# Pooling as a product with a constant band matrix, lambda by a small matmul, and another place for the residual affine

## The chip, the cores and the metric

One core of one Trainium2 chip runs the whole program. The metric is the device time of one execution in microseconds (us); lower is better. The kernel before was run three times for its median, and once more under the hardware profiler.

## The reference

A diffusion backbone of two layers works on 256 latent tokens and 256 context tokens of 1024 channels. Each layer is a half-step SwiGLU feed-forward, a token mixer, and a second feed-forward; after each of them the residual goes through a LayerNorm with gain and bias. Layer 0 mixes with differential attention plus multi-scale pooling, layer 1 with a convolution. What the change touches is in the mixer of layer 0:

```python
lam = exp(sum(lam_q1 * lam_k1)) - exp(sum(lam_q2 * lam_k2)) + lam_init      # one number
z_lat = h_lat @ w_in                       # q, k, v: 512 columns each, then u: 512 columns
# pooling of u, four groups of 128 channels, windows 2, 4, 8, 16 over the tokens:
mean = (csum[hi] - csum[lo]) / (hi - lo)   # windowed mean, clipped at both ends
pooled = mean - u                          # per group
y = pooled @ w_pool[g] * pool_scale
# attention: p_diff = softmax(s0) - lam * softmax(s1);  out = p_diff @ v
```

## The kernel before, in words

Every large product is made three times (mm3, lines 194 to 197: high x high, high x low, low x high), with each operand split into a rounded high part (fp32r) and its remainder. Activations lie split and transposed in XH and XL, as [channel, token]: tokens 0 to 255 are latent, 256 to 511 context. Weights come from HBM as fp32 in 1 MB jobs into three raw buffers (pump_load, queue SP), and each job is cut into pieces of 128x1024 that ScalarE copies to wh and VectorE subtracts to wl (pump_split, lines 132 and 133). Six pairs of wh and wl rotate; wnext (line 136) takes the next piece and asks for those up to five ahead.

The feed-forward ahead of the mixer ends with four blocks of 128 tokens in a row, t = 0, 1 (latent) and 2, 3 (context). Each ends in finish(t), lines 579 to 584: LayerNorm without its gain and bias (they are folded into the next modulation), then to_x, which transposes h[t] on TensorE (tile tra), modulates it on VectorE and ScalarE (xma), and splits it into XH and XL. The second half of each XL split is on GpSimd (line 333). For the latent tokens the gain and bias still have to be applied to the residual h[t] itself: affine(t, 0, 0, pool), put aside in a list (later, line 584) and emitted when flush is called. It loads two rows of 1024 floats to all partitions by GpSimd's own DMA queue, through one buffer, and multiplies and adds them in halves: for two blocks four row loads and eight 128x512 operations, all issued on GpSimd.

The mixer (lines 591 to 822) takes u first: four products of 256 columns (lines 626 to 629) give u as [channel, token], ScalarE copies each into the zero-padded tile UP, and GpSimd forms the windowed sums SA and SB by shifted additions, multiplies with INV (1 / count), subtracts u, and splits the result into PH and PL (lines 630 to 642; the last instruction is called pooled). Lambda (lines 605 to 614) is a product and a reduction on VectorE over a loaded tile lq, then an exponential on ScalarE. Then come, as written, four q heads and two k heads, each with a rotation (rope, lines 644 to 658: ScalarE copy rh, a matmul with perm, VectorE products t1 and t2, a ScalarE copy and a VectorE subtraction), attend(0), the product for v, attend(1), and so on. PH and PL are read much later, by the product with w_pool (lines 769 to 776). flush(pooled) stands at line 805, after attend_out(3).

The order of each engine's queue is made by a planner at build time: on each engine it takes the earliest-written instruction among those that are ready, unless an edge holds one back. tc.issue_after(i) makes such edges: it queues the instructions of its block behind instruction i, those of i's own engine only. (behind_x, line 274, therefore opens it for two anchors, a VectorE and a ScalarE one, to hold both halves of a weight split.) The engines then run their queues strictly in order. Memory of a closed pool is reused: the mixer's pools mp and m2 lie where the feed-forward's pools lay, and their tiles wait for the last reader there.

Of the kernel before, what the change touches and what calls it, by code (L numbers as in the profile page):

```python
# [9 lines left out]
F32 = mybir.dt.float32  # L10
# [6 lines left out]
P = 128  # L17
# [25 lines left out]
CO = {}  # L43
_n = 0
for _name, _w in (("c", 8), ("cc", 8), ("lng", 48), ("lnb", 48), ("cvg", 8), ("cvb", 8), ("bc1", 16), ("bdw", 8),
                  ("psc", 4), ("sub", 1), ("bad", 9 * 8 * DEPTH)):
    CO[_name] = _n
    _n += _w
NCOL = _n
# [3 lines left out]
def body(ctx: ExitStack, tc: tile.TileContext, out, a):  # L53
# [13 lines left out]
    def mmt(name):  # L67
        return mmp.tile([P, 512], F32, tag="mm", name=name)
# [30 lines left out]
    def w_add(src, widths):  # L99
        jobs.append((src, widths))  # L100
# [61 lines left out]
    PARTS4 = ((0, 8), (8, 16), (16, 22))  # L162
    PARTS2 = ((0, 22),)
    add_ffn(0, 0, 4, PARTS4)
    for g in range(2):
        w_add(a["wu"][2 * g:2 * g + 2].rearrange("j p f -> p j f"), (1024, 1024))
    for hd in range(0, NH, 2):
        w_add(a["wqk"][0, hd:hd + 2].rearrange("j p f -> p j f"), (1024, 1024))
    w_add(a["wqk"][1, 0:2].rearrange("j p f -> p j f"), (1024, 1024))
    for hh in range(2):  # L170
        w_add(a["wv"][:, hh * 2048:(hh + 1) * 2048], (1024, 1024))
    w_add(a["wqk"][1, 2:4].rearrange("j p f -> p j f"), (1024, 1024))
# [418 lines left out]
    with ExitStack() as st2:  # L591
        mp = st2.enter_context(tc.tile_pool(name="mp", bufs=1))
        m2 = st2.enter_context(tc.tile_pool(name="m2", bufs=2))
        xmp[:] = m2, 2
        UP = mp.tile([P, 4, 512], F32R, tag="VH", name="UP").bitcast(F32)[:, :, 0:272]
        pool.memset(UP, 0.0)
        cosT = mp.tile([P, SEQ], F32, name="cosT")
        nc.sync.dma_start(cosT, a["cosT"])
        sinT = mp.tile([P, SEQ], F32, name="sinT")
        nc.sync.dma_start(sinT, a["sinT"])  # L600
        perm = mp.tile([P, P], F32, name="perm")
        nc.sync.dma_start(perm, a["perm"])
        INV = m2.tile([P, 4, SEQ], F32, tag="pt", bufs=4, name="INV")
        nc.sync.dma_start(INV, a["inv"].partition_broadcast(P))
        lq = m2.tile([P, 4, 64], F32, tag="rh", name="lq")
        nc.sync.dma_start(lq, a["lam"].partition_broadcast(P))
        lam = mp.tile([P, 4], F32, name="lam")
        dve.tensor_tensor(lq[:, 0:2, :], lq[:, 0:2, :], lq[:, 2:4, :], ALU.mult)
        dve.tensor_reduce(lam[:, 0:2], lq[:, 0:2, :], AX.X, ALU.add)
        act.activation(lam[:, 0:2], lam[:, 0:2], AF.Exp)  # L610

        dve.tensor_tensor(lam[:, 2:3], lam[:, 1:2], lam[:, 0:1], ALU.subtract)
        lam_init = 0.8 - 0.6 * math.exp(-0.3 * 0)
# [4 lines left out]
        def proj(ps, tok0, tok1):  # L618
            wh, wl = wnext()
            for k in range(KT):  # L620
                mm3(ps, wh[:, k * P:(k + 1) * P], wl[:, k * P:(k + 1) * P], XH[:, k, tok0:tok1], XL[:, k, tok0:tok1],
                    k == 0, k == KT - 1)

        SA = m2.tile([P, 4, 272], F32, tag="pt", bufs=4, name="SA")
        SB = m2.tile([P, 4, 272], F32, tag="pt", bufs=4, name="SB")
        for g in range(4):
            psu = mmt(f"u{g}")[:, 0:SEQ]
            proj(psu, 0, SEQ)
            act.copy(UP[:, g, 8:8 + SEQ], psu)
        pool.tensor_tensor(SA[:, :, 0:271], UP[:, :, 0:271], UP[:, :, 1:272], ALU.add)  # L630
        pool.tensor_tensor(SB[:, 1:4, 0:269], SA[:, 1:4, 0:269], SA[:, 1:4, 2:271], ALU.add)
        pool.tensor_tensor(SA[:, 2:4, 0:265], SB[:, 2:4, 0:265], SB[:, 2:4, 4:269], ALU.add)
        pool.tensor_tensor(SB[:, 3, 0:257], SA[:, 3, 0:257], SA[:, 3, 8:265], ALU.add)
        PH = mp.tile([P, 4, SEQ], F32R, tag="PH", name="PH")
        PL = mp.tile([P, 4, SEQ], F32R, tag="PL", name="PL")
        for g, win in enumerate(WINS):
            src = (SA, SB)[g % 2]
            o = 8 - win // 2
            pool.tensor_tensor(INV[:, g, :], src[:, g, o:o + SEQ], INV[:, g, :], ALU.mult)
            pool.tensor_tensor(INV[:, g, :], INV[:, g, :], UP[:, g, 8:8 + SEQ], ALU.subtract)  # L640
# [48 lines left out]
        def attend(hd, between=None):  # L689
# [25 lines left out]
            if between is not None:  # L715
                with tc.issue_after(between().ins):
                    for qt in range(2):
                        turn(hd, qt, es[qt])

        def turn(hd, qt, e):  # L720
            pth, ptl = PT[hd]
            qs = slice(qt * P, (qt + 1) * P)
            tr = trt(f"ptr{hd}{qt}")
            for kt in range(4):
                pe.transpose(tr[:, kt * P:(kt + 1) * P], e[:, 0, kt * P:(kt + 1) * P], ident)
            split(pth[:, :, qs], ptl[:, :, qs], tr.rearrange("p (k q) -> p k q", k=4))

        def attend_out(hd):
            pth, ptl = PT[hd]
# [29 lines left out]
            do_q(hd)  # L759
        do_k(0)  # L760
        do_k(1)
        attend(0)
        do_v()
        attend(1)
        do_k(2)
# [36 lines left out]
        attend_out(2)  # L802
        pooled_half(1)
        attend_out(3)
        flush(pooled)
        for n in range(2):
            for q in range(2):
                wq[q, n] = wnext()
# [236 lines left out]
def _layout(i):  # L1045
    import numpy as np
    f = lambda v: np.asarray(v)
    ar = np.ascontiguousarray
    L = DEPTH
    o = {}  # L1050

    def vec(v):
        return f(v).reshape(-1, P).T

    b_ada = f(i["b_ada"]).reshape(L, 9, D)

    GATES = (2, 5, 8)
    by = lambda b, v: b.reshape(P, 8).T if v in GATES else b.reshape(8, P)
    bad = np.concatenate([by(b_ada[l, v], v).T for l in range(L) for v in range(9)], axis=1)
    o["cols"] = ar(np.concatenate([  # L1060
        vec(i["c"]), vec(i["c_ctx"]), vec(i["ln_g"]), vec(i["ln_b"]), vec(i["conv_ln_g"]), vec(i["conv_ln_b"]),
        vec(i["b_c1"]), vec(i["b_dw"]), vec(i["pool_scale"]), vec(i["subln_g"]), bad], axis=1))
    o["wdw"] = ar(f(i["w_dw"])[0].reshape(TAPS, 8, P).transpose(2, 1, 0).reshape(P, 8 * TAPS))
    x, ctx = f(i["x"])[0], f(i["ctx"])[0]
    o["x"], o["ctx"] = ar(x), ar(ctx)
    o["xT"] = ar(np.stack([v.reshape(SEQ, KT, P).transpose(2, 1, 0).reshape(P, KT * SEQ) for v in (x, ctx)]))
    wa = f(i["w_ada"]).reshape(L, D, 9, D)
    o["wst"] = ar(wa[0, :, 0:2].reshape(2, 4, P, 2, 2, 512).transpose(3, 4, 0, 2, 1, 5).reshape(2, 2, 2, P, 2048))
    wt = wa.transpose(0, 2, 3, 1)
    o["wada"] = ar(np.stack([np.stack([  # L1070
        wt[l, v].reshape(P, 8, D).transpose(1, 0, 2) if v in GATES else wt[l, v].reshape(8, P, D)
        for v in range(9)]) for l in range(L)]))
    o["c_row"], o["cc_row"] = ar(f(i["c"])[0]), ar(f(i["c_ctx"]))
    o["ln_g"], o["ln_b"] = ar(f(i["ln_g"])), ar(f(i["ln_b"]))
# [8 lines left out]
    o["wu"] = ar(wm[:, 1536:].reshape(KT, P, 4, P).transpose(2, 1, 0, 3).reshape(4, P, 1024))  # L1083
# [7 lines left out]
    o["lam"] = ar(np.stack([f(i["lam_" + k])[0] for k in ("q1", "q2", "k1", "k2")]))  # L1091

    f4 = np.float32
    pos = np.arange(SEQ)
    inv = (f4(10000.0) ** (-np.arange(16, dtype=f4) / f4(16))).astype(f4)
    ang = np.stack([(pos // 64).astype(f4)[:, None] * inv, (pos % 64).astype(f4)[:, None] * inv], 1)
    tab = lambda v: ar(np.broadcast_to(v.astype(f4).transpose(1, 2, 0)[None, :, None], (2, 2, 2, 16, SEQ)).reshape(P, SEQ))
    o["cosT"], o["sinT"] = tab(np.cos(ang)), tab(np.sin(ang))
    perm = np.zeros((P, P), f4)
    for m in range(P):  # L1100
        if m % 32 < 16:
            perm[m + 16, m] = -1.0
        else:
            perm[m - 16, m] = 1.0
    o["perm"] = perm
    cnt = np.stack([np.clip(pos - w // 2 + w, 0, SEQ) - np.clip(pos - w // 2, 0, SEQ) for w in WINS])
    o["inv"] = (1.0 / cnt).astype(f4)
    return o


# [14 lines left out]
```

## Time and profile before

| | us |
|---|---|
| median of three runs | 1262.07 (1261.28 to 1267.06) |
| the profiled execution | 1265.42 |
| its span in the profile | 1263.6 |
| TensorE busy in the span | 1213.8 (96%) |
| VectorE busy | 893.3 (71%) |
| ScalarE busy | 520.0 (41%) |
| GpSimd busy | 250.3 (20%) |

Times in the rows are us from the start of the span. PE is TensorE, PEld its weight load, DVE VectorE, ACT ScalarE, POOL GpSimd, SPq the queue that issues most DMAs. In a row of the timeline the bracket at the end says how long the engine had been idle before the instruction, and which instruction ended that. The mixer of layer 0 runs from about 403 to 538.

### The profile page before, as it was taken

The page shows a single profiled execution, that of the slowest core. Times are in us where ns is not written, and L with a number is a line of the kernel's source. Part 1 is how long each engine was busy: PE and PEld are TensorE (multiplying, and loading weights), DVE is VectorE, ACT ScalarE, POOL GpSimd, SP SyncE. Part 2 cuts the span into 40 slices and gives each one's busy share as a digit, 9 for nine tenths or more (in the row PEclk, how much of TensorE's full clock was granted, in tenths as well). Part 3 has the DMA queues.
Part 4 walks back from the last instruction along what each step waited for, and adds up shares of the span by engine and source line. Part 5 has one row for each costly group of instructions (what it writes and reads, how often), then busy time and mean ns, then how long its engine had stood idle before and what let it go on. Part 6 is the DMA issues. An engine that isn't in the chain of part 4 may idle for free.

```text
span 1263.6 us, 17520 instructions
## 1 busy us (share of the span) xinstructions
PE 1213.8 (96%) x6886; PEld 1037.2 (82%) x6886; DVE 893.3 (71%) x1278; ACT 520.0 (41%) x790; POOL 250.3 (20%) x231
## 2 busy tenths in 40 slices
PE   7999999999999899989999999999999979999997
PEld 1788888888887777779998869999879867999985
DVE  6889987733328957787785668888658976775554
ACT  2533122212323535553444443444438853444430
POOL 0010201111003740123000014201016961420000
PEclk9999999999999999989999999999999989999999
DMA  9797788632231452558985649998726042875550
GB/s 366 286 370 252 276 283 291 232 100 99 80 117 67 140 166 67 167 188 299 327 291 184 238 144 333 321 333 307 260 105 240 22 146 117 309 269 176 180 183 34
DMA packets 63748, 264.32 MB, mean 209 GB/s; under 512 B 5937, under 2 KB 6705, under 8 KB 56241
## 3 DMA queue, kind: packets, MB, share of 16 engines
q1 hardware_dynamic: 60128, 251.11, 56.8%
q0 software_dynamic: 3536, 12.09, 3.1%
q8 instruction: 54, 0.88, 0.3%
q14 instruction: 30, 0.24, 0.1%
HBM read 262.10 MB, written 1.08 MB: 208 GB/s over the span
## 4 chain that ended last, share of the span: by engine, by line
PE 84%; DVE 8%; ACT 3%; DMA 2%; issue 1%; POOL 1%; SPq 0%; DVEq 0%; ACTq 0%; POOLq 0%
PE of L197 8%; PE of L196 8%; PE of L195 8%; PE uf L197 8%; PE uf L196 8%; PE uf L195 8%; PE gf L196 7%; PE gf L195 7%; PE gf L197 7%; PE c L197 1%; DVE wl L133 1%; PE c L196 1%; PE c L195 1%; PE pc L986 1%; PE st L519 1%
## 5 line engine op out<-in xcount | busy, mean ns | idle before, releaser
L133 DVE TENSOR_TENSOR wl<-raw,wh 128x1024 fp32r<-128x1024 f32 x298 | 376.5, 1276 | 170.9 <-ACT wh L132 170.0
L132 ACT CAST wh<-raw 128x1024 fp32r<-128x1024 f32 x313 | 321.9, 1048 | 394.7 <-PE of L197 130.0
L197 PE MATMUL uf<-XH,wl 128*128 128x256 f32 (+1 forms) x656 | 205.2, 313 | 1.9 <-DVE wl L133 1.9
L195 PE MATMUL uf<-XH,wh 128*128 128x256 f32 (+1 forms) x656 | 205.0, 312 | 0.0
L196 PE MATMUL uf<-XL,wh 128*128 128x256 f32 (+1 forms) x656 | 205.0, 312 | 0.0
L195 PE MATMUL gf<-XH,wh 128*128 128x256 f32 (+1 forms) x656 | 204.6, 312 | 0.3 <-ACT XH L202 0.3
L196 PE MATMUL gf<-XL,wh 128*128 128x256 f32 (+1 forms) x656 | 204.5, 312 | 0.0
L197 PE MATMUL gf<-XH,wl 128*128 128x256 f32 (+1 forms) x656 | 204.5, 312 | 0.0
L237 DVE SCALAR_TENSOR_TENSOR ada<-ada,crow0ada 128x1024 f32<-128x1024 f32 x104 | 137.3, 1332 | 71.0 <-DMA ada<-in_wada 71.0
L196 PE MATMUL of<-wl,GHf 128*128 128x512 f32 x344 | 136.5, 397 | 0.0
L197 PE MATMUL of<-wh,GLf 128*128 128x512 f32 x344 | 136.4, 397 | 0.0
L195 PE MATMUL of<-wh,GHf 128*128 128x512 f32 x344 | 136.4, 396 | 0.0
L197 PEld LDWEIGHTS uf<-XH,wl 128*128 128x128 f32 x656 | 125.9, 192 | 9.0 <-DVE wl L133 2.1
L195 PEld LDWEIGHTS gf<-XH,wh 128*128 128x128 f32 x656 | 125.2, 191 | 8.6 <-issue 0.9
L195 PEld LDWEIGHTS uf<-XH,wh 128*128 128x128 f32 x656 | 126.0, 192 | 6.9
L196 PEld LDWEIGHTS uf<-XL,wh 128*128 128x128 f32 x656 | 125.9, 192 | 6.8
L196 PEld LDWEIGHTS gf<-XL,wh 128*128 128x128 f32 x656 | 125.1, 191 | 7.3 <-DVE XL L202 0.4
L197 PEld LDWEIGHTS gf<-XH,wl 128*128 128x128 f32 x656 | 125.2, 191 | 6.8
L245 POOL TENSOR_TENSOR m<-m,cols 128x8 f32<-128x8 f32 x19 | 16.4, 862 | 331.3 <-DVE ada L237 209.1
L196 PEld LDWEIGHTS of<-wl,GHf 128*128 128x128 f32 x344 | 64.8, 188 | 15.8 <-DVE wl L133 0.2
L197 PEld LDWEIGHTS of<-wh,GLf 128*128 128x128 f32 x344 | 64.8, 188 | 15.7
L195 PEld LDWEIGHTS of<-wh,GHf 128*128 128x128 f32 x344 | 64.8, 188 | 15.5
(293 smaller groups left out, 1858.6 us busy)
## 6 DMA issues: line engine op xcount, KB each, us to landing
raw<-in_wfi SPq DMA_DIRECT2D x82, 1024.0 KB, 6.8
ada<-in_wada SPq DMA_DIRECT2D x128, 512.0 KB, 5.4
raw<-in_wfo SPq DMA_DIRECT2D x40, 1024.0 KB, 4.9
raw<-in_wc SPq DMA_DIRECT2D x10, 1024.0 KB, 5.2
aw<-in_wst SPq DMA_DIRECT2D x16, 512.0 KB, 7.7
raw<-in_wfl SPq DMA_DIRECT2D x6, 1024.0 KB, 5.2
raw<-in_wfo SPq DMA_DIRECT2D x8, 512.0 KB, 3.5
raw<-in_wqk SPq DMA_DIRECT2D x4, 1024.0 KB, 5.1
```

Source lines behind the costliest of these rows:

```text
L132: act.copy(wh[:, :w], r[:, off:off + w])
L133: lo_ins[q] = (pool if q in pool_lo else dve).tensor_tensor(wl[:, :w], r[:, off:off + w], wh[:, :w].bitcast(F32), ALU.subtract)
L195: pe.matmul(ps, lh, rh, start=first, stop=False)
L196: pe.matmul(ps, lh, rl, start=False, stop=False)
L197: last_mm[0] = pe.matmul(ps, ll, rh, start=False, stop=last)
L237: dve.scalar_tensor_tensor(st["raw"] if s == streams[-1] else crow["junk"], st["raw"], 1.0, crow[s], ALU.mult, ALU.mult, accum_out=mcol[l, ...
L245: pool.tensor_tensor(m, m, col("bad", (l * 9 + v) * 8, 8), ALU.add)
L519: started = pe.matmul(ps[0:2, :], scv[:, :, k], src, start=started is None, stop=not dq and k == KT - 1)
L986: last = pe.matmul(pc, dg, zp[:, j, tap:tap + SEQ], start=tap == 0, stop=tap == TAPS - 1)
```

## The change

The pooling becomes a product. For each group the matrix of windowed mean minus identity, 256 x 256, is a constant input (band, two 128x1024 pieces, one more 1 MB weight job between the first two k heads and v). u is made as [token, channel], two products of 512 columns with X as the stationary operand, each split by ScalarE and VectorE into U. pooling() multiplies U with band: 8 calls of mm3, 24 matmuls of 256 columns, into two PSUM tiles, which are split into PH and PL. It is called inside attend(0), between the scores and the transposes of the probabilities, which are queued behind its last matmul.

The four lambda vectors come as columns of the tile cols that is loaded at the start; VectorE multiplies them, a matmul with a tile of ones sums over the partitions, ScalarE takes the exponential from PSUM.

flush moves from line 805 (after attend_out(3), behind pooled) to behind attend(0), with the last VectorE half of a probability split (turned[0]) as its anchor. GpSimd's fourteen pooling instructions, the memset of UP and the loads of INV and lq go; a memset of ones comes.

```diff
-    for g in range(2):
-        w_add(a["wu"][2 * g:2 * g + 2].rearrange("j p f -> p j f"), (1024, 1024))
+    for hh in range(2):
+        w_add(a["wu"][:, hh * 2048:(hh + 1) * 2048], (1024, 1024))
...
     w_add(a["wqk"][1, 0:2].rearrange("j p f -> p j f"), (1024, 1024))
+    w_add(a["band"].rearrange("j p f -> p j f"), (1024, 1024))
...
-        lq = m2.tile([P, 4, 64], F32, tag="rh", name="lq")
-        nc.sync.dma_start(lq, a["lam"].partition_broadcast(P))
+        ones = m2.tile([P, P], F32, tag="rh", name="ones")
+        pool.memset(ones, 1.0)
         lam = mp.tile([P, 4], F32, name="lam")
-        dve.tensor_tensor(lq[:, 0:2, :], lq[:, 0:2, :], lq[:, 2:4, :], ALU.mult)
-        dve.tensor_reduce(lam[:, 0:2], lq[:, 0:2, :], AX.X, ALU.add)
-        act.activation(lam[:, 0:2], lam[:, 0:2], AF.Exp)
+        lp = m2.tile([P, 2], F32, tag="mx", name="lp")
+        dve.tensor_tensor(lam[:, 3:4], col("lam", 0), col("lam", 1), ALU.mult)
+        dve.tensor_scalar(lp, col("lam", 2, 2), lam[:, 3:4], None, ALU.mult)
+        lps = trt("lps")[:, 0:2]
+        pe.matmul(lps, ones, lp, start=True, stop=True)
+        act.activation(lam[:, 0:2], lps, AF.Exp)
...
-        for g in range(4):
-            psu = mmt(f"u{g}")[:, 0:SEQ]
-            proj(psu, 0, SEQ)
-            act.copy(UP[:, g, 8:8 + SEQ], psu)
-        pool.tensor_tensor(SA[:, :, 0:271], UP[:, :, 0:271], UP[:, :, 1:272], ALU.add)
...
-        pool.tensor_copy(PH, INV)
-        pooled = pool.tensor_tensor(PL, INV, PH.bitcast(F32), ALU.subtract)
+        U = mp.tile([P, 2, 2, 512], F32R, tag="VH", name="U")
+        ws = [wnext() for _ in range(4)]
+        for t in range(2):
+            psu = mmt(f"u{t}")
+            for k in range(KT):
+                out_mm(psu, t, XH, XL, 0, k, k % 2, ws[k // 2], k == 0, k == KT - 1)
+            split(U[:, 0, t, :], U[:, 1, t, :], psu)
...
+        def pooling():
+            ws = [wnext(), wnext()]
+            for g2 in range(2):
+                pp = mmt(f"pp{g2}")
+                for j in range(2):
+                    g = 2 * g2 + j
+                    gs = slice(g * P, (g + 1) * P)
+                    bs = slice(g * SEQ, (g + 1) * SEQ)
+                    for t in range(2):
+                        wh, wl = ws[t]
+                        mm3(pp[:, j * SEQ:(j + 1) * SEQ], U[:, 0, t, gs], U[:, 1, t, gs], wh[:, bs], wl[:, bs], t == 0, t == 1)
+                gs = slice(2 * g2, 2 * g2 + 2)
+                split(PH[:, gs, :], PL[:, gs, :], pp.rearrange("p (j t) -> p j t", j=2))
+            return last_mm[0]
...
-            split(pth[:, :, qs], ptl[:, :, qs], tr.rearrange("p (k q) -> p k q", k=4))
+            turned[0] = split(pth[:, :, qs], ptl[:, :, qs], tr.rearrange("p (k q) -> p k q", k=4))[1]
...
-        attend(0)
+        attend(0, pooling)
+        flush(turned[0])
         do_v()
...
         attend_out(3)
-        flush(pooled)
```

## Rows read from the trace of the kernel before

**Rows 1.** Page, part 1: engine, busy us (share), instructions.
```profile
PE 1213.8 (96%) x6886; PEld 1037.2 (82%) x6886; DVE 893.3 (71%) x1278; ACT 520.0 (41%) x790; POOL 250.3 (20%) x231
```

**Rows 2.** Page, part 4: the chain that ended last, by engine.
```profile
PE 84%; DVE 8%; ACT 3%; DMA 2%; issue 1%; POOL 1%; SPq 0%; DVEq 0%; ACTq 0%; POOLq 0%
```

**Rows 3.** Windows: from:to, length, busy us of each engine, clock, DMA share, GB/s.
```profile
402.69:418.51 15.82, 14.25 (x113) 13.43 (x113) 13.65 (x25) 10.01 (x18) 7.23 (x5) 1.00 0.36 107
418.51:428.18 9.67, 9.67 (x78) 9.26 (x76) 8.59 (x9) 6.95 (x12) 7.17 (x4) 1.00 0.97 322
428.18:434.49 6.31, 3.59 (x27) 3.49 (x28) 6.10 (x11) 1.99 (x5) 6.23 (x8) 1.00 0.30 106
434.49:445.00 10.51, 7.12 (x26) 5.42 (x25) 9.73 (x12) 2.45 (x5) 7.28 (x6) 0.84 0.22 53
454.46:477.90 23.44, 23.16 (x108) 18.62 (x106) 12.30 (x22) 8.11 (x15) 9.06 (x8) 1.00 0.48 158
```

**Rows 4.** Timeline of PE: start, length, operation, out and in, shape, [idle before].
```profile
402.69 0.67 PE L195 MATMUL u<-XH,wh 128*128 128x256 f32 x4
...
412.15 1.13 PE L325 MATMUL tra<-ident,h 128*128 128x128 f32 x8
...
430.90 1.13 PE L648 MATMUL rotq<-rhq,perm 128*128 128x256 f32 x4 [2.72 <-ACT rhq L646]
...
439.88 1.22 PE L648 MATMUL rotq<-rhq,perm 128*128 128x256 f32 x2 [3.39 <-ACT rhq L646]
...
444.20 0.39 PE L195 MATMUL k<-XH,wh 128*128 128x512 f32 x1
444.43 0.40 PE L196 MATMUL k<-XL,wh 128*128 128x512 f32 x1
...
454.46 0.50 PE L195 MATMUL v<-wh,XH 128*128 128x512 f32 x1
```

**Rows 5.** Windows of one microsecond, same columns as group 3.
```profile
441.00:442.00 1.00, 1.00 (x4) 0.81 (x3) 1.00 (x1) 0.00 (x0) 0.92 (x2) 0.50 0.00 0
```

**Rows 6.** Timeline of ACT, same columns as group 4.
```profile
430.07 0.20 ACT L610 ACTIVATE lam<-lam 128x2 f32<-128x2 f32 x1 [2.75 <-DVE lam L609]
...
473.95 0.59 ACT L202 CAST VH<-v 128x512 fp32r<-128x512 f32 x1 [0.36 <-PE v L197]
```

**Rows 7.** Groups by line and form, 402.69 to 454.46: busy us, mean ns, idle before.
```profile
L133 DVE TENSOR_TENSOR wl<-raw,wh 128x1024 fp32r<-128x1024 f32 x12 | 20.8, 1737 | 2.9 <-ACT wh L132 2.9
```

**Rows 8.** Instructions of tile wl, whole span: min/median/max ns.
```profile
L133 DVE TENSOR_TENSOR wl<-raw,wh x298: 728/1222/3367, 31.8 to 1239.7; 128x1024 fp32r<-128x1024 f32 x148, 128x512 fp32r<-128x512 f32 x1
```

**Rows 9.** Timeline of DVE, same columns as group 4.
```profile
426.02 1.75 DVE L650 TENSOR_TENSOR rt1q<-rhq,cosT 128x256 f32<-128x256 f32 x1
...
443.00 0.41 DVE L650 TENSOR_TENSOR rt1q<-rhq,cosT 128x256 f32<-128x256 f32 x1
...
475.87 0.69 DVE L202 TENSOR_TENSOR VL<-v,VH 128x512 fp32r<-128x512 f32 x1 [0.43 <-ACT VH L202]
```

**Rows 10.** Timeline of POOL, same columns as group 4.
```profile
406.14 1.69 POOL L202 TENSOR_TENSOR XL<-xma,XH 128x512 fp32r<-128x512 f32 x1 [2.12 <-ACT XH L202]
...
420.77 1.29 POOL L202 TENSOR_TENSOR XL<-xma,XH 128x512 fp32r<-128x512 f32 x1 [4.42 <-ACT XH L202]
422.14 2.88 POOL L630 TENSOR_TENSOR SA<-UP 128x1084 f32<-128x1084 f32 x1
...
438.92 2.40 POOL L642 TENSOR_TENSOR PL<-INV,PH 128x1024 fp32r<-128x1024 f32 x1
441.27 0.64 POOL L358 DMA_DIRECT2D ln_g<-in_ln_g  x1
446.14 3.53 POOL L361 TENSOR_TENSOR h<-h,ln_g 128x512 f32<-128x512 f32 x2 [4.22 <-DMA ln_g<-in_ln_g]
...
470.10 2.55 POOL L361 TENSOR_TENSOR h<-h,ln_b 128x512 f32<-128x512 f32 x2 [4.92 <-DMA ln_b<-in_ln_b]
...
525.54 0.19 POOL L746 TENSOR_SCALAR ss<-ss 128x2 f32<-128x2 f32 x1 [5.72 <-ACT on L744]
```

More of the change, by code (lines that the diff above doesn't have):

```diff
@@ L45 @@
 for _name, _w in (("c", 8), ("cc", 8), ("lng", 48), ("lnb", 48), ("cvg", 8), ("cvb", 8), ("bc1", 16), ("bdw", 8),
-                  ("psc", 4), ("sub", 1), ("bad", 9 * 8 * DEPTH)):
+                  ("psc", 4), ("sub", 1), ("lam", 4), ("bad", 9 * 8 * DEPTH)):
     CO[_name] = _n
@@ L594, in body @@
         xmp[:] = m2, 2
-        UP = mp.tile([P, 4, 512], F32R, tag="VH", name="UP").bitcast(F32)[:, :, 0:272]
-        pool.memset(UP, 0.0)
         cosT = mp.tile([P, SEQ], F32, name="cosT")
@@ L602, in body @@
         nc.sync.dma_start(perm, a["perm"])
-        INV = m2.tile([P, 4, SEQ], F32, tag="pt", bufs=4, name="INV")
-        nc.sync.dma_start(INV, a["inv"].partition_broadcast(P))
-        lq = m2.tile([P, 4, 64], F32, tag="rh", name="lq")
-        nc.sync.dma_start(lq, a["lam"].partition_broadcast(P))
+        ones = m2.tile([P, P], F32, tag="rh", name="ones")
+        pool.memset(ones, 1.0)
         lam = mp.tile([P, 4], F32, name="lam")
-        dve.tensor_tensor(lq[:, 0:2, :], lq[:, 0:2, :], lq[:, 2:4, :], ALU.mult)
-        dve.tensor_reduce(lam[:, 0:2], lq[:, 0:2, :], AX.X, ALU.add)
-        act.activation(lam[:, 0:2], lam[:, 0:2], AF.Exp)
+        lp = m2.tile([P, 2], F32, tag="mx", name="lp")
[4 more added lines that the diff above has]
+        act.activation(lam[:, 0:2], lps, AF.Exp)
         dve.tensor_tensor(lam[:, 2:3], lam[:, 1:2], lam[:, 0:1], ALU.subtract)
@@ L622, in proj @@
                     k == 0, k == KT - 1)
-        SA = m2.tile([P, 4, 272], F32, tag="pt", bufs=4, name="SA")
-        SB = m2.tile([P, 4, 272], F32, tag="pt", bufs=4, name="SB")
-        for g in range(4):
-            psu = mmt(f"u{g}")[:, 0:SEQ]
-            proj(psu, 0, SEQ)
-            act.copy(UP[:, g, 8:8 + SEQ], psu)
-        pool.tensor_tensor(SA[:, :, 0:271], UP[:, :, 0:271], UP[:, :, 1:272], ALU.add)
[L631 to L640, printed above, removed]
-        pool.tensor_copy(PH, INV)
-        pooled = pool.tensor_tensor(PL, INV, PH.bitcast(F32), ALU.subtract)
+        U = mp.tile([P, 2, 2, 512], F32R, tag="VH", name="U")
[5 more added lines that the diff above has]
+            split(U[:, 0, t, :], U[:, 1, t, :], psu)
+        PH = mp.tile([P, 4, SEQ], F32R, name="PH")
+        PL = mp.tile([P, 4, SEQ], F32R, name="PL")
+        def pooling():
[12 more added lines that the diff above has]
+            return last_mm[0]
         def rope(ps, dh, dl, scale, name):
@@ L718, in attend @@
                         turn(hd, qt, es[qt])
+        turned = [None]
         def turn(hd, qt, e):
@@ L1059, in _layout @@
     bad = np.concatenate([by(b_ada[l, v], v).T for l in range(L) for v in range(9)], axis=1)
+    pair = lambda u, v: np.concatenate([f(i["lam_" + u])[0], f(i["lam_" + v])[0]])
+    half = np.repeat(np.eye(2, dtype=np.float32), 64, axis=0)
+    lam = np.stack([pair("q1", "q2"), pair("k1", "k2"), half[:, 0], half[:, 1]], axis=1)
     o["cols"] = ar(np.concatenate([
         vec(i["c"]), vec(i["c_ctx"]), vec(i["ln_g"]), vec(i["ln_b"]), vec(i["conv_ln_g"]), vec(i["conv_ln_b"]),
-        vec(i["b_c1"]), vec(i["b_dw"]), vec(i["pool_scale"]), vec(i["subln_g"]), bad], axis=1))
+        vec(i["b_c1"]), vec(i["b_dw"]), vec(i["pool_scale"]), vec(i["subln_g"]), lam, bad], axis=1))
     o["wdw"] = ar(f(i["w_dw"])[0].reshape(TAPS, 8, P).transpose(2, 1, 0).reshape(P, 8 * TAPS))
@@ L1082, in _layout @@
     o["wqk"] = ar(wm[:, 0:1024].reshape(KT, P, 2, NH, P).transpose(2, 3, 1, 0, 4).reshape(2, NH, P, 1024))
-    o["wu"] = ar(wm[:, 1536:].reshape(KT, P, 4, P).transpose(2, 1, 0, 3).reshape(4, P, 1024))
+    o["wu"] = ar(wm[:, 1536:].reshape(KT, P, 512).transpose(1, 0, 2).reshape(P, KT * 512))
     o["wpool"] = ar(f(i["w_pool"])[0].transpose(1, 0, 2).reshape(P, 512))
@@ L1090, in _layout @@
     o["b_c2"] = ar(f(i["b_c2"]))
-    o["lam"] = ar(np.stack([f(i["lam_" + k])[0] for k in ("q1", "q2", "k1", "k2")]))
     f4 = np.float32
@@ L1105, in _layout @@
     o["perm"] = perm
-    cnt = np.stack([np.clip(pos - w // 2 + w, 0, SEQ) - np.clip(pos - w // 2, 0, SEQ) for w in WINS])
-    o["inv"] = (1.0 / cnt).astype(f4)
+    band = []
+    for w in WINS:
+        lo, hi = np.clip(pos - w // 2, 0, SEQ), np.clip(pos - w // 2 + w, 0, SEQ)
+        m = ((pos[:, None] >= lo) & (pos[:, None] < hi)).astype(np.float64) / (hi - lo)
+        band.append((m - np.eye(SEQ)).astype(f4).reshape(2, P, SEQ))
+    o["band"] = ar(np.stack(band, axis=2).reshape(2, P, 4 * SEQ))
     return o
```

## The prediction, made before the changed kernel was run

> **What bounds the kernel now.** I began with the page's busy shares: TensorE is busy 96% of the span [rows 1], and in the chain that ended last it holds 84%, VectorE 8%, GpSimd 1% [rows 2]. So an edit pays where TensorE idles or runs at half clock, and time added to TensorE's queue is paid in full. Next I cut the mixer's front into windows [rows 3], from TensorE's first matmul for u at 402.69 to its first for v at 454.46 [rows 4]: 51.77 us, the stretch that the change rewrites. The reader should see three losses there. While u is made, 15.82 - 14.25 = 1.57 us of idle [rows 3]. In front of two rotation matmuls, 2.72 and 3.39 us, both waiting for ScalarE's copy rhq [rows 4]. And half clock after the second: the mean granted clock is 0.84 over 10.51 us [rows 3], one microsecond of it at 0.50 [rows 5]; 0.16 x 10.51 = 1.7 us of full-clock work is missing. Together 1.57 + 6.11 + 1.7 = 9.4 us are to be had. From the first v on there is little: 23.16 of 23.44 us busy [rows 3].
>
> Then I asked who makes rhq late. For the first idle it is ScalarE itself: lambda's exponential sat 2.75 us waiting for VectorE's reduction of lq, with rhq queued behind it [rows 6]. For the second it is VectorE, busy 13.65 + 8.59 + 6.10 + 9.73 = 38.07 of the 42.31 us up to 445 [rows 3], and slow: twelve weight splits took 1737 ns on average [rows 7] where the median of all 298 is 1222 [rows 8], and a rotation product took 1.75 us at 426.02, while GpSimd was pooling, and 0.41 at 443.00, when it was not [rows 9]. GpSimd was busy 7.23 + 7.17 + 6.23 + 7.28 = 27.9 us in the same four windows [rows 3]. The excess that I can count is 12 x 0.515 + 1.34 = 7.5 us, or 0.27 us of VectorE for each us of GpSimd.
>
> **The change part by part.** *u as [token, channel].* 48 matmuls of 512 columns, 0.23 us apart [rows 4], are 11.0 us; the 96 of 256 columns that go are, at 9.67 / 78 = 0.124 us [rows 3], 11.9. The second figure has rotation matmuls in it, so I take the two as equal. The order matters more: the old products need both latent blocks from the start, the new first one only block 0. Block 1's XL split ends on GpSimd at 406.14 + 1.69 = 407.8 [rows 10]; the first product covers 24 x 0.23 + 1.13 of a transpose group [rows 4] = 6.6 us, to 409.3. Of the 1.57 us I let 0.3 stay. All four weight pieces are wanted within the first product, but were asked for five ahead, so I cost that at nothing; without this cover, up to one split of 1.22 [rows 8].
>
> Here a rule of the Trainium skill is weighed. The rows say 0.23 us between matmuls of 512 columns [rows 4]. "TensorE: Matmul & The Clock Gate", section Back-to-back issue gap, gives about 131 ns each for a sustained stream with weight loads; by it u would take an estimated 48 x 0.131 = 6.3 us and the change gain 4.7 us more. These rows contradict it; it is the last rival.
>
> *Band product.* 24 matmuls x 0.124 = 3.0 us, on TensorE's path in full: in the old stretch v's matmuls already fill the wait for the softmax, so this product hides nothing. *Lambda.* One matmul of two columns: between 0 and 0.28 us (four wider rotation matmuls take 1.13 [rows 4]); I take 0.1. It needs a memset of ones in memory that is free only after block 3's XL split (420.77 + 1.29 [rows 10]). It is a new wait in TensorE's queue, with q's matmuls queued behind it; between 0 and 2.7 us, the old lambda wait moved; I take 0, as two VectorE operations on single columns stand in for the loaded lq. The old wait of 2.72 goes.
>
> *VectorE.* Added in the stretch: two U splits at 0.69 (the V split out of PSUM [rows 9]) and two band splits at 1.22 [rows 8], 3.8 us; two splits of the product come after the scores, beside v, where VectorE has 12.30 of 23.44 us busy [rows 3]. ScalarE gets the same splits, 0.59 us for one out of PSUM [rows 6], and is busy 21.4 of the 42.31 us [rows 3], so it has room. Removed: pooling, 422.14 to 441.3 on GpSimd [rows 10], 19.2 us x 0.27 = 5.2 us of slowing.
>
> *The affine.* This is where I doubt the change. Before, flush is written behind attend_out(3), whose GpSimd step runs at 525.54, yet the row load is issued at 441.27, the moment that PL (438.92 + 2.40) is done [rows 10]: only the edge to pooled held it, and the planner pulled it 84 us ahead. The new anchor turned[0] is a VectorE instruction, the affine is all GpSimd's, and issue_after orders the anchor's own engine only. So nothing holds it, and I expect it not beside v but as soon as h[0] and h[1] have been transposed, ahead of and inside the u products. Its four rounds took 441.27 to 472.65 [rows 10]; its pairs took 2.55 to 3.53 us, so some 12 us of GpSimd, which slow VectorE by 12 x 0.27 = 3.2 us in a fuller place. Two pairs, some 6.3 us, were inside the old stretch, so 1.7 goes. Its four DMAs are GpSimd's own queue and load the same bytes as before.
>
> Balance of VectorE: +3.8 + 3.2 - 5.2 - 1.7 = +0.1 us. So it is not relieved, and is asked to do the same in a shorter stretch. I keep 2.7 of the 3.39 us of idle, the bounds being 0 and 3.39. After the idle of 2.72 the clock stayed at 1.00, after 3.39 it fell [rows 3]; with 2.7 I keep no loss there, the bounds being 0 and 1.7.
>
> *DMA.* One more 1 MB job, with 0.22 to 0.97 of the DMA engines busy [rows 3] and v's weights due later; nothing, or up to 1 us if SP's queue, where it is in front of v's weights, falls behind.
>
> **The sum.** Gone 9.4 - 0.3 - 2.7 = 6.4; added 3.0 + 0.1 = 3.1; gain 3.3 us. Against the profiled execution: 1265.42 - 3.3 = 1262.1. That execution lies 3.35 above the median of the runs; the losses are waits inside the core that I take to be in both, so the forecast is 1262.07 - 3.3 = 1258.8, stated as 1259.
>
> **The rivals.** (a) *The cover is complete*: the affine falls into GpSimd's gaps and VectorE keeps up. Then 2.7 more goes: 1256. For it: the excess ratio is an average, and the affine's first pair can run before the stretch. Against: the balance above. (b) *The change does not do what it says*: VectorE stays the bound, the ropes lag as before, and 6.1 + 1.7 + 0.3 us stay lost while 3.1 is added: 1262.07 - 9.4 + 8.1 + 3.1 = 1264. For it: 90% busy now. (c) *Slower*: GpSimd's queue is in order, and a round of the affine (0.64 issue, 4.22 wait, 3.53 for the pair: 8.4 us [rows 10]) stands ahead of block 1's XL split. Then that split ends at 407.8 + 8.4 = 416.2, and the second u product, wanted at 409.3, waits 6.9 us, the clock falls (1.7), and 2.7 + 0.3 stay: 9.4 - 11.6 - 3.1 = -5.3, so 1267. It decides from a wait of 3.3 us on. Against: to_x has priority, so it needs a row that lands later than the planner thought. (d) *The faster issue* of the rule above would give 1254; the rows leave it almost nothing.
>
> **How the numbers follow.** Forecast 0.50, (a) 0.22, (b) 0.16, (c) 0.10, (d) 0.02. Range 1253.5 to 1266: below it (d) and the luckier part of (a), above it most of (c); some 0.15 is left out. About 0.5%, 6.3 us, is what a measurement of this kernel can tell from no change. Faster than 1255.8: half of (a), a tail of the forecast, (d): 0.20. Slower than 1268.4: the worse part of (c) and a tail of (b): 0.08. Within: 0.72.
>
> **What would show it.** The stretch from the first u to the first v, 51.77 us before, should be about 48.5. In front of the second u product there should be no idle. The affine's row loads should be issued before 420; if they come after the scores, my reading of the anchor is wrong and (a) is near. Weight splits between 402 and 440 should average about 1.5 us, not 1.74. No idle should be put down to lambda. Wrong would be a gain outside this stretch, above all at the end of the mixer, where I change nothing.

## The result, and the profile after

The changed kernel takes 1269.52 us (median of 11 runs, 1267.67 to 1277.45) where the kernel before takes 1262.19 us beside it (11 runs, 1260.35 to 1267.06). The ratio is 1.0055, with a 95% interval of 1.0037 to 1.0074: slower by some 7 us, outside the range of 1253.5 to 1266. The likeliest case was wrong in its sign; the side that came true is rival (c), and its time, 1267, was close.

The profiled execution of after has a span of 1268.6 us against 1263.6 before. I cut both at the same first instructions. The page of after, part 1 (engine, busy us, share, instructions), answering [rows 1]:

```profile
PE 1217.5 (96%) x6864; PEld 1037.2 (82%) x6864; DVE 887.0 (70%) x1284; ACT 523.4 (41%) x792; POOL 231.8 (18%) x217
```

GpSimd has 18.5 us less to do, and yet the kernel is slower. The chain that ended last cannot be set beside [rows 2]: in after it runs through loads of ada (5% of the span), which the change does not touch, and its shares add up to only 68%. The timeline of PE in after (start, length, operation, out and in, shape, [idle before and its releaser]), answering [rows 4]:

```profile
38.47 0.50 PE L196 MATMUL gf<-XH,wh 128*128 128x512 f32 x1
...
406.40 1.94 PE L326 MATMUL tra<-ident,h 128*128 128x128 f32 x8 [3.91 <-issue]
...
411.90 0.39 PE L198 MATMUL of<-wh,GLf 128*128 128x512 f32 x1
412.13 0.40 PE L196 MATMUL u<-wh,XH 128*128 128x512 f32 x1
...
423.29 1.13 PE L326 MATMUL tra<-ident,h 128*128 128x128 f32 x8 [2.47 <-ACT XH L203]
...
434.05 0.35 PE L609 MATMUL lps<-lp,ones 128*128 128x2 f32 x2 [2.04 <-POOL ones L603]
...
460.22 0.39 PE L196 MATMUL pp<-wh,U 128*128 128x256 f32 x1
...
463.19 0.40 PE L196 MATMUL v<-wh,XH 128*128 128x512 f32 x1
...
549.93 0.50 PE L196 MATMUL lf<-wh,XH 128*128 128x512 f32 x1 [3.56 <-ACT XH L203]
```

The reader should see that the two idles of [rows 4] ahead of the query rotations are gone, and that others stand in their place, the largest ahead of the stretch that I had studied. In before, the first large matmul (gf) and the first of the next block (lf), which [rows 4] do not show, stand here:

```profile
35.10 0.50 PE L195 MATMUL gf<-XH,wh 128*128 128x512 f32 x1
...
541.34 0.50 PE L195 MATMUL lf<-wh,XH 128*128 128x512 f32 x1 [3.43 <-ACT XH L202]
```

The windows of after, same columns as [rows 3] (from:to, length, busy of PE, PEld, DVE, ACT, POOL, clock, DMA share, GB/s), answering those rows:

```profile
0.00:38.50 38.50, 28.46 (x65) 5.35 (x65) 22.67 (x52) 8.55 (x14) 1.40 (x7) 0.96 0.97 369
...
406.40:412.10 5.70, 5.70 (x19) 4.88 (x20) 4.55 (x10) 1.89 (x4) 2.23 (x2) 0.57 0.29 100
...
434.30:445.00 10.70, 10.70 (x71) 10.40 (x72) 8.28 (x17) 5.42 (x9) 0.00 (x0) 0.84 0.60 196
```

After the idle of 3.91 us the granted clock is 0.57 over 5.7 us, and after lambda's 2.04 it is 0.84 over 10.7: 2.5 and 1.7 us of full-clock work missing.

By place, from the two timelines: TensorE's first large matmul (gf) starts at 38.47 instead of 35.10, +3.4. From there to the first u it takes 373.66 instead of 367.59, +6.1. From the first u to the first v, 51.06 instead of 51.77, -0.7: that was to be -3.3. From the first v to the first matmul of the next block (lf) 86.74 against 86.88. The rest, lf to the end, is 3.6 shorter in after; the mean clock from 541.3 to 934.1 was 0.99 before and is 1.00 after, and the profiled execution of before lies 3.35 above its own median, so I do not count that to the change. Without it the sum is 8.6 for the two profiled executions, 7.3 between the medians.

What holds TensorE up ahead of the first u is read from GpSimd's timeline of after (same columns), answering [rows 10]:

```profile
1.28 0.70 POOL L359 DMA_DIRECT2D ln_g<-in_ln_g  x1 [0.35 <-issue]
...
396.03 2.54 POOL L362 TENSOR_TENSOR h<-h,ln_g 128x512 f32<-128x512 f32 x2 [1.38 <-PE tra L326]
398.87 0.64 POOL L359 DMA_DIRECT2D ln_b<-in_ln_b  x1 [0.30 <-POOL h L362]
400.68 1.28 POOL L203 TENSOR_TENSOR XL<-xma,XH 128x512 fp32r<-128x512 f32 x1 [1.17 <-DVE XL L203]
402.71 2.48 POOL L362 TENSOR_TENSOR h<-h,ln_b 128x512 f32<-128x512 f32 x2 [0.76 <-DMA ln_b<-in_ln_b]
405.15 0.57 POOL L306 TENSOR_TENSOR rsf<-rsf,mhalf 128x1 f32<-128x1 f32 x1
405.68 0.74 POOL L359 DMA_DIRECT2D ln_g<-in_ln_g  x1
409.89 2.44 POOL L362 TENSOR_TENSOR h<-h,ln_g 128x512 f32<-128x512 f32 x1 [3.47 <-DMA ln_g<-in_ln_g]
412.31 0.55 POOL L306 TENSOR_TENSOR rsf<-rsf,mhalf 128x1 f32<-128x1 f32 x1
...
418.57 3.51 POOL L362 TENSOR_TENSOR h<-h,ln_b 128x512 f32<-128x512 f32 x2 [0.84 <-DMA ln_b<-in_ln_b]
422.04 0.56 POOL L306 TENSOR_TENSOR rsf<-rsf,mhalf 128x1 f32<-128x1 f32 x1
```

rsf is the small power that ends each block's normalization: h is scaled with it, transposed (tra) and split. It takes 0.57 us, but it stands in GpSimd's queue behind an affine instruction that waits for a row. VectorE's timeline of after (same columns) shows when its operand is ready, and who waits for it:

```profile
401.39 0.14 DVE L305 TENSOR_SCALAR rsf<-mvf 128x1 f32<-128x1 f32 x1
...
405.76 1.00 DVE L313 TENSOR_SCALAR h<-h,mvf,rsf 128x512 f32<-128x512 f32 x2 [3.63 <-POOL rsf L306]
...
433.70 0.25 DVE L607 TENSOR_SCALAR lp<-cols,lam 128x2 f32<-128x2 f32 x1 [1.16 <-POOL XL L203]
```

The operand is ready at 401.53, and GpSimd comes to the power at 405.15, 3.6 us later: behind an XL split, 0.76 us of waiting for a row, and 2.48 us of the affine's own work. The instruction at 405.76 is followed by the transposes at 406.40, behind their 3.91 us of idle. And the first row is loaded at 1.28 us, at the start of the program. The last line, lambda's product, is for later.

### The profile page after: what moved, and what is told of

Same layout as the page of the kernel before. It is cut to its first block, busy times and chain, and to the rows that moved or that the text cites. A ratio compares the mean times of both kernels' runs of the same rounds, so it can differ in the third digit from the quotient of the medians.

```text
span 1268.6 us, 17470 instructions
## 1 busy us (share of the span) xinstructions
PE 1217.5 (96%) x6864; PEld 1037.2 (82%) x6864; DVE 887.0 (70%) x1284; ACT 523.4 (41%) x792; POOL 231.8 (18%) x217
## 4 chain that ended last, share of the span: by engine, by line
PE 46%; DVE 9%; DMA 6%; issue 3%; ACT 2%; POOL 2%; DVEq 0%; SPq 0%; POOLq 0%; ACTq 0%
DMA ada<-in_wada 5%; PE of L197 4%; PE of L198 4%; PE of L196 4%; PE gf L197 3%; PE gf L198 3%; PE gf L196 3%; PE uf L198 3%; PE uf L197 3%; PE uf L196 3%; DVE wl L133 2%; DVE ada L238 2%; PE pc L994 1%; PE c L196 1%; PE c L198 1%
```

## Experiments

Theories. *Order*: the freed affine, by its place in GpSimd's queue and by its early row load, costs what was lost, and the product for pooling pays as forecast. *Work*: the products themselves (two-step u, band product, lambda matmul) cost more than they give. All ratios below stand against the kernel before, run beside it on the same chip; "us" for a ratio is its distance from 1, times 1262.

**1. The change with the affine held back** until attend(0)'s exponentials are summed, by an anchor on GpSimd itself.

```
-        flush(turned[0])
+        hold = mp.tile([P, 1], F32, name="hold")
+        flush(pool.tensor_copy(hold, R1[0][:, 1:2]))
```

> The changed kernel with one edit: the residual affine is queued behind a small GpSimd copy that reads a result of attend(0), so that it really runs beside the product for v, and its first row load cannot go to the start of the program. Order theory (the whole loss comes from where the unheld affine lands: 3.4 us at the start, some 6 us in front of u): the first matmul for u comes back to about 403 us, no idle of TensorE over 1.2 us between the end of the feed-forward and q, time 1256 to 1260. Work theory (the loss is the product's own work, 24 matmuls, splits, one more weight job): the time stays at 1267 to 1270.

Measured 1262.39 us, ratio 0.9990 (0.9975 to 1.0006). Both losses ahead of u are gone: gf at 35.5, first u at 403.1. So the order costs 0.0065 +- 0.0025 of the time (the two half-widths as a root of squares), 8.2 us. But the time expected was not reached: the change in good order only equals the kernel before. What is left to lose shows in three places. Its timeline of PE:

```profile
423.34 0.35 PE L609 MATMUL lps<-lp,ones 128*128 128x2 f32 x2 [2.06 <-POOL ones L603]
```

Its timeline of POOL:

```profile
420.00 2.96 POOL L203 TENSOR_TENSOR XL<-xma,XH 128x512 fp32r<-128x512 f32 x1 [4.17 <-ACT XH L203]
423.01 0.20 POOL L603 MEMSET ones<- 128x128 f32 x1
```

And a window of 5 us, columns as above, the clock third from the end:

```profile
423.00:428.00 5.00, 4.66 (x26) 4.63 (x27) 4.30 (x9) 3.18 (x5) 0.20 (x1) 0.68 0.36 102
```

The ones that lambda's matmul sums with are filled on GpSimd only when block 3's XL split ends at 422.96; TensorE waits 2.06 us, and the clock is 0.68 behind it.

**2. The kernel before with the affine freed**: emitted behind attend(0) with no anchor, old pooling, old lambda.

```
         attend(0)
+        while later:
+            later.pop(0)()
...
-        flush(pooled)
```

> The kernel before with one edit: the affine is emitted behind attend(0) without an anchor, so that the planner may place it as in the changed kernel; pooling stays on GpSimd, u and lambda as before. Order theory: the two losses appear here too, 3.4 us at the start and 4 to 6 us in front of u, time 1268 to 1273. Work theory: 1260 to 1264.

Measured 1274.00 us, ratio 1.0082 (1.0061 to 1.0104), 1 us above the range expected. The losses of after appear without any of its arithmetic: gf at 36.8, first u at 410.3, 4.3 us of idle ahead of a group of transposes. Order, again.

**3. The order, taken apart.** Four kernels. *row_late* is the change with only the first row load kept from the start: the anchor is the FFN's last residual add on GpSimd, and all else runs as early as in after. *before_row* is the kernel before with that one load moved to the start and the affine left where it was. *start2* is the kernel before with two 512 KB loads at the start that nobody reads. *rows_once* is the change with one row, loaded in the FFN, in place of all four, so that the eight instructions run early with no row to wait for; three loads are left out, and the gain is added where the bias belongs.

row_late:

```
-        flush(turned[0])
+        flush(last_res[0])
```

before_row:

```
+        row0 = rowp.tile([P, D], F32, tag="lnrow", name="ln_g000")
+        pool.dma_start(row0, a["ln_g"][0, 0].partition_broadcast(P))
```

start2:

```
+        for key in ("ln_g", "ln_b"):
+            extra = sp.tile([P, D], F32, name=f"extra{key}")
+            pool.dma_start(extra, a[key][0, 0].partition_broadcast(P))
```

rows_once:

```
+            if (l, i) == (0, 0):
+                row = rows0[0]
```

> The changed kernel with only the first row load kept from the start: the affine is queued behind GpSimd's last residual addition of the feed-forward, the rest of it lies in GpSimd's queue as in the changed kernel. Order theory: the first large matmul comes back from 38.5 to about 35.1 us, the stalls in front of u stay (u from about 408 us), time 1265 to 1267. If the later start has nothing to do with the row load: 1269 to 1270 and the first large matmul at 38.5.

> The kernel before with only the affine's first row load freed (it then stands near the head of GpSimd's queue); all else of the affine stays behind the pooling. Order theory: the first large matmul moves from 35.1 to about 38.5 us and the time is 1264 to 1266. If the later start has nothing to do with the row load: 1261 to 1263.

> The kernel before with two more row loads of 512 KB on GpSimd's queue at the very start, into tiles that nothing reads; all else unchanged. If a row load at the start costs its bytes on a path that waits for data there: the first large matmul moves from 35.1 to 37.5 to 39 us (twice the 1.5 us of one load), time 1264 to 1268. If the start of the changed kernel was late for another reason: 1261 to 1263.

> The changed kernel with the affine as early as in it, but without any row load among its steps: one row is loaded in the middle of the feed-forward and serves all eight operations (the gain row is added in place of the bias row; three of the four row loads are left out). If the stall in front of u comes from waits for rows in GpSimd's queue: the idle in front of the transposes is under 2 us in all and the time within 2 us of held, 1261 to 1264. If it comes from GpSimd operations standing ahead of the LayerNorm's power and the XL splits, whatever they wait for: idle of 4 us and more stays in front of the transposes, time 1265 to 1268.

Measured: row_late 1267.47 us, 1.0039 (1.0024 to 1.0055), gf back at 35.4, but 4.2 us of idle ahead of a group of transposes. before_row 1266.93 us, 1.0031 (1.0017 to 1.0044), gf at 36.6, where 38.5 was expected. start2 1266.88 us, 1.0040 (1.0025 to 1.0055), gf at 37.3. rows_once 1264.14 us, 1.0018 (1.0004 to 1.0033). The timeline of POOL of rows_once:

```profile
392.72 5.94 POOL L366 TENSOR_TENSOR h<-h,ln_g 128x512 f32<-128x512 f32 x4 [1.38 <-PE tra L326]
...
401.80 6.54 POOL L366 TENSOR_TENSOR h<-h,ln_g 128x512 f32<-128x512 f32 x4 [1.40 <-PE tra L326]
408.31 0.54 POOL L306 TENSOR_TENSOR rsf<-rsf,mhalf 128x1 f32<-128x1 f32 x1
```

Four instructions of the affine still stand ahead of the power at 408.31. The largest of the waits of PE in rows_once (what waits, for what: us in total, times, longest):

```profile
PE tra L326 <- issue: 5.0, 2, 3.1
```

So rows_once fell between its two expectations: its time is within 2 us of held, as the one for waits said, and its idle is 5 us, as the one for instructions said. Both have a part.

before_row tells less of the load than it was made for. With the row in place, the affine's first pair no longer waits 4.22 us for it behind PL, as at 446.14 in [rows 10], but runs at once, beside the rotations. Its timelines of POOL, DVE and PE, and its window from the first u to the first v:

```profile
442.82 3.70 POOL L365 TENSOR_TENSOR h<-h,ln_g 128x512 f32<-128x512 f32 x2
...
443.87 1.51 DVE L662 SCALAR_TENSOR_TENSOR ql<-rt1q,qh 128x256 fp32r<-128x256 f32 x1
...
448.98 0.70 PE L652 MATMUL rotk<-rhk,perm 128*128 128x256 f32 x2 [1.85 <-ACT rhk L650]
...
404.20:458.10 53.90, 45.67 (x281) 39.45 (x280) 45.24 (x64) 25.80 (x48) 35.28 (x27) 0.94 0.42 141
```

TensorE waits 1.85 us ahead of a key rotation, and the stretch is 2.1 us longer than the 51.77 of before. With the 1.5 us at gf that is 3.6 of the 3.9 us that before_row costs, so less than half of its price is seen at the load.

So the 8.2 us have three parts, each a difference of timed kernels and good to about 2.8 us. The load at the start: 2.0 us by after less row_late (0.0016, an interval that reaches past zero); start2, whose rows nobody reads, shows on its own that loads there cost time, 5.0 us (3.2 to 6.9) for two. The affine's instructions ahead of the normalization's powers: 0.0028, 3.5 us, by rows_once less held. Its waits for rows: the rest of row_late less held (0.0049, 6.2 us), 2.7 us, again not clear of zero by itself. The profiled executions give the same order: the first v starts at 452.41 in held, 455.46 in rows_once and 458.83 in row_late, all with gf at 35.2 to 35.5, and at 463.19 in after.

**4. The start once more.** In one execution of the kernel before with the new lambda (experiment 5), which has no early load, gf stood at 38.2 too, with half clock ahead of it. So after and that kernel were each profiled once more, unchanged.

> The changed kernel once more, for its start. If its late first large matmul (38.5 us against 35.1) with a half clock at 26 us belongs to the row load at the start, the first large matmul stands at 37 us or later again. If the half clock there is chance of one execution, it stands at 36 to 37 us, 1 to 2 us behind the kernel before, without a half clock ahead of it.

> The kernel before with the new lambda alone once more, for its start: it has no row load there, and yet its first large matmul stood at 38.2 us with a half clock at 26 us. If that was chance of one execution, the first large matmul stands at 35 to 36 us now. If the four added columns or anything else of the new lambda make the start late, it stands at 37 us or later again.

Measured: gf at 38.7 in after, with half clock again (0.91 over the first 20 us); 36.2 in the other, with full clock. The half clock lies between 15 and 19 us in all three executions that have it, not at 26 as the two expectations say. Of all kernels here, the four that load a row at the start (five executions) have gf at 36.6 to 38.7; the eight without (nine executions) at 35.0 to 36.2, but for that one of 38.2. So the half clock at the start can come without the load, and the load can come without it: before_free, before_row and start2 hold the full clock there, with gf at 36.6 to 37.3. That the load makes it likelier rests on the two of two in after alone, and is not shown.

**5. Lambda and the product, each alone.** *held_ones* is experiment 1 with the ones filled at the start of the program and lp in memory of its own. *before_lam* is the kernel before with the new lambda only; *before_lam_ones* the same with the ones filled early. *held_oldlam* is experiment 1 with the old lambda: the band product, with the affine held.

held_ones and before_lam_ones:

```
+    ones = const.tile([P, P], F32, name="ones")
+    pool.memset(ones, 1.0)
...
-        lp = m2.tile([P, 2], F32, tag="mx", name="lp")
+        lp = mp.tile([P, 2], F32, name="lp")
```

held_oldlam:

```
-        lps = trt("lps")[:, 0:2]
-        pe.matmul(lps, ones, lp, start=True, stop=True)
-        act.activation(lam[:, 0:2], lps, AF.Exp)
+        dve.tensor_tensor(lq[:, 0:2, :], lq[:, 0:2, :], lq[:, 2:4, :], ALU.mult)
+        dve.tensor_reduce(lam[:, 0:2], lq[:, 0:2, :], AX.X, ALU.add)
+        act.activation(lam[:, 0:2], lam[:, 0:2], AF.Exp)
```

> The kernel of run held, and in it the tile of ones lies in constant memory and is set at the start, and lp lies in mp, so that the lambda matmul no longer waits for memory that the last XL split frees. If the wait of 2.06 us in front of the lambda matmul is real time on TensorE's path: no idle there, the half-clock stretch that follows it gone too, and 2 to 4 us less than held (1257 to 1260 beside a kernel before of 1262). If the ropes behind it would have made TensorE wait for the same memory anyway: the idle moves to the first rotation matmul and the time stays within 1 us of held.

> The kernel before with the new lambda alone (columns, matmul with ones, exponential from PSUM); pooling, affine and u as before. My forecast's step: the idle of 2.72 us in front of a rotation matmul goes, nothing takes its place, 1259 to 1261. The rival: the lambda matmul waits in TensorE's queue for ones as it does in held (2.1 us), and the time is the same as before, 1261 to 1264.

> The kernel before with the new lambda alone, its ones matrix in memory of its own that is filled at the start of the program and its product in memory of its own: nothing of lambda waits for GpSimd between h and u any more. If the wait of TensorE for the two small operations (4.7 us in the kernel with the new lambda alone) and the half clock behind it are the whole price of the new lambda, this one takes 1261 to 1264 us, ratio 0.999 to 1.002, and no idle stands ahead of lps. If the price came from the four added columns or from anything else that the small matmul brings, it stays at 1266 to 1270 us.

> The pooling as a product and the affine behind the residual adds of GpSimd, with lambda as in the kernel before: the band product alone. If the product gains some 3 us and the wait of the small lambda matmul gave 2 to 3 of them back, this takes 1258 to 1261 us, ratio 0.997 to 0.999, like the kernel with the ones matrix filled early, and the stretch from the first u to the first v is 47 to 48 us. If the gain of that kernel came from the earlier ones alone and the product itself brings nothing, it stays at 1262 to 1264 us.

Measured: held_ones 1260.09 us, 0.9975 (0.9963 to 0.9987), 1.9 us better than held with an interval that reaches past zero. before_lam 1268.78 us, 1.0052 (1.0038 to 1.0066), above both of its expectations. before_lam_ones 1265.04 us, 1.0014 (1.0001 to 1.0026), the median 1 us over what was expected for the wait as the whole price. held_oldlam 1258.68 us, 0.9968 (0.9957 to 0.9978): like held_ones it beats both kernels, and it is the product without the new lambda. Its window from the first u to the first v:

```profile
403.00:450.30 47.30, 44.23 (x257) 36.90 (x256) 38.38 (x75) 28.30 (x53) 7.72 (x6) 1.00 0.38 127
```

Its waits of PE from 395 to 480:

```profile
PE rotq L651 <- ACT rhq L649: 1.4, 2, 0.9
PE tra L326 <- ACT XH L203: 1.2, 1, 1.2
```

Its timeline of POOL:

```profile
398.19 0.56 POOL L306 TENSOR_TENSOR rsf<-rsf,mhalf 128x1 f32<-128x1 f32 x1
...
451.14 0.66 POOL L359 DMA_DIRECT2D ln_g<-in_ln_g  x1
...
484.75 3.51 POOL L362 TENSOR_TENSOR h<-h,ln_b 128x512 f32<-128x512 f32 x2 [3.29 <-DMA ln_b<-in_ln_b]
```

47.3 us instead of 51.77, at full clock, with 1.4 us of idle left ahead of the query rotations; rsf at 398.19 where after had 405.15 (3.1 us of the difference from the start); the affine's four rounds at 451 to 488, beside the products for v.

Two things in it I had not looked for. The old wait of 2.72 us is gone although the old lambda is still there: on ScalarE a second copy rhq now stands ahead of lambda's exponential, where in before it was queued behind the one of [rows 6].

```profile
425.98 0.37 ACT L649 COPY rhq<-q 128x256 f32<-128x256 f32 x1
...
428.83 0.20 ACT L607 ACTIVATE lam<-lam 128x2 f32<-128x2 f32 x1
```

And 1.6 of the 4.5 us are lost again behind the first v. The windows from the first v to lf, of before and of held_oldlam, and a wait of PE in the second, where before waited 0.60 us:

```profile
454.46:541.34 86.88, 79.55 (x399) 61.88 (x397) 61.10 (x121) 46.80 (x106) 13.44 (x17) 1.00 0.38 127
450.30:538.80 88.50, 79.44 (x399) 61.79 (x397) 66.22 (x116) 47.08 (x104) 20.82 (x22) 1.00 0.43 149
...
481.26 0.63 PE L730 MATMUL ptr<-ident,e 128*128 128x128 f32 x4 [2.60 <-DVE c L713]
```

VectorE and GpSimd are busier there by 5.1 and 7.4 us: the affine now runs beside this part.

What the new lambda alone does (6.6 us) is read from the second execution of before_lam. Its timeline of PE:

```profile
426.05 0.35 PE L612 MATMUL lps<-lp,ones 128*128 128x2 f32 x2 [4.71 <-DMA INV<-in_inv]
```

Its timeline of DVE:

```profile
421.67 2.30 DVE L133 TENSOR_TENSOR wl<-raw,wh 128x1024 fp32r<-128x1024 f32 x1
423.89 1.95 DVE L610 TENSOR_SCALAR lp<-cols,lam 128x2 f32<-128x2 f32 x1
```

Its timeline of POOL:

```profile
422.95 0.20 POOL L606 MEMSET ones<- 128x128 f32 x1
423.11 2.71 POOL L633 TENSOR_TENSOR SA<-UP 128x1084 f32<-128x1084 f32 x1
```

The releaser named is a DMA, but lp ends at 425.84 and lps starts at 426.05: lp is what came last. It multiplies two columns, starts only behind a weight split of 2.30 us, and takes 1.95 us beside the pooling's sum SA, where it takes 0.25 in after. The stretch from the first u to the first v is 54.3 us there, and from the first v to lf it is 88.6: 2.5 and 1.7 us more than before. Where the rest of the 6.6 us lies is not shown.

With the ones filled early and lp moved, 4.8 of the 6.6 us come back (1.0052 less 1.0014, good to 2.4 us); which of the two moves did it was not tried. And the small matmul still waits, against what was expected. Its row and a window of 5 us in before_lam_ones:

```profile
419.24 0.38 PE L612 MATMUL lps<-lp,ones 128*128 128x2 f32 x2 [1.67 <-ACT xma L333]
...
419.24:424.24 5.00, 5.00 (x29) 5.00 (x30) 2.85 (x5) 3.98 (x7) 3.12 (x2) 0.66 0.90 328
```

It takes its PSUM tile from the same few as the transposes, and now waits for one that ScalarE has still to read (xma); in held_ones it waits 0.5 us in the same way.

## Why the prediction was wrong, point by point

**The affine, the step that failed.** I read the anchor rightly: nothing holds the affine, and its row loads go out before 420. But I priced it as GpSimd's work that slows VectorE, 3.2 us less 1.7 in the old stretch, and wrote its loads down as "GpSimd's own queue and load the same bytes as before", at nothing. That is counting what is moved and not what it is moved past. The loads went past the whole FFN to the program's start; the four rounds went ahead of three normalization powers, in an in-order queue, three of them behind a wait for a row (0.76, 3.47 and 0.84 us). Measured: 8.2 us. I also looked for it in the wrong place, from the first u on: the losses lie ahead of the first u, while TensorE still ends the FFN.

**Rival (c)** had this mechanism, a round of the affine in GpSimd's queue ahead of what u needs, at 0.10. Its time was right to 2.5 us, its details were not: what holds TensorE is not block 1's XL split, but the power from which h itself is made. So the near time is partly luck: rival (c) kept 2.7 us ahead of the rotations that are gone in after, and had neither the 3.4 us at the start nor lambda's wait. I had argued against it that the transposes' side has priority. In the queue that gave nothing: an instruction that waits for its row keeps all behind it.

**Lambda's wait**, taken at 0 between 0 and 2.7. It is 2.04 us in after and 2.06 in held, with half clock behind it; held less held_oldlam is 0.0022 +- 0.0019, 2.8 us. I had written down the memset and when its memory comes free (422.06), and the query products queued behind; with both known, the price of zero had no row behind it. Nor was the new lambda needed to end the old wait of 2.72: held_oldlam has the old lambda and no such wait. "No idle should be put down to lambda" is false in after.

**The product.** The 24 matmuls run from 460.22 to 463.19, 3.0 us, as forecast. u's order brought next to nothing: 1.2 us of idle stay in held_oldlam ahead of block 3's transposes, inside the second u product, where I let 0.3 stay. VectorE I had too slow: 1.4 us of the 6.11 of idle stay, where I kept 2.7, and the half clock is gone. In all the product with the affine held gives 4.0 us (2.8 to 5.4) where the sum said 3.3, and 1258.7 where the forecast said 1259. So the sum came out for the parts in it, partly because errors offset each other (less idle stays at the rotations, more inside u, and 1.6 us are lost behind the first v, which it did not have), and the forecast was that of another kernel: this one with the old lambda and with the affine held. Order (8.2) and lambda's wait (2.8), less the 0.7 that the product gave beyond the sum, are 10.3 of the 10.5 us by which the time missed 1259.

**Rivals (a), (b), (d).** (a) is what VectorE did in held_oldlam, nearly: without affine and pooling in the stretch, it keeps up, at 38.38 of 47.30 us busy. (b), VectorE still the bound, is refuted: in after no idle stands ahead of a query rotation, and in held_oldlam 1.4 us of the 6.11 are left. (d), the rule of the Trainium skill ("TensorE: Matmul & The Clock Gate", Back-to-back issue gap) of about 131 ns, is not seen here: the matmuls of 512 columns at 411.90 and 412.13 are again 0.23 us apart.

**The signs I named.** Stretch of about 48.5 us: 51.1, and 47.3 in held_oldlam. Weight splits between 402 and 440 at about 1.5 us: nine in 11.84 us in after, 1.32 each; my 1.74 of before ran on to 454, and over the same window the eleven of before took 16.29 us, 1.48 each, so this sign hardly told the two kernels apart. The rate of 0.27 has the same slip in it: its splits run on to 454 and its GpSimd time stops at 445; with the 4.51 us in between it is 7.5 / 32.4 = 0.23. No idle ahead of the second u product: there is none, but 2.47 us inside it, ahead of block 3's transposes. "A gain outside this stretch" would be wrong: it was a loss there, 9.5 us in the two profiled executions, and I had not named that.

## What to carry to other kernels

When an anchor is removed or moved to another engine, list every instruction that it held, loads included, and go back in that engine's queue to the earliest point at which nothing else holds them; price what stands behind them there, from who needs the result to TensorE, not only the work they bring. An in-order queue makes a wait for a load a wait for all that follows, so a small step that a long path needs (here a power of 0.57 us) is the first thing to look for behind it. A small constant or product in memory that comes free just before its use is a wait like any other; with both in memory of their own, and the constant filled at the start, 4.8 us came back in the kernel before and 1.9 us, not clear of zero, in held.

## What the runs showed of the hardware that I had not expected

- A VectorE instruction on two columns took 1.95 us beside a GpSimd addition, and 0.25 us without one. In both executions of before_lam it ended within 0.03 us of that addition (425.84 and 425.82, 427.80 and 427.77). So the slowing that I had used as a rate on large tiles does not go by length here: it looks as if this instruction had waited for the addition to end.
- One 512 KB load ahead of the first weights, with the DMA engines 0.97 busy over the first 38.5 us, costs by its bytes an estimated 0.52 MB / 369 GB/s = 1.4 us; gf came 1.5 us later in before_row. The timed difference of 3.9 us (2.1 to 5.6) is larger because the early row also let the affine run earlier. For two loads that nobody reads, gf came 2.2 us later and the timed difference is 5.0 us (3.2 to 6.9); what lies between these two the runs leave open.
- An idle of 2.06 us on TensorE was followed by a clock of 0.68 over the next 5 us in held, and one of 1.67 us by 0.66 in before_lam_ones, where in [rows 3, 4] an idle of 2.72 us was followed by none. The length of one idle alone did not decide it here.
